# The first queries' low products in full width, and two pieces of W_out in each other's ring

## The chip, the cores and the metric

The kernel runs on one core of a Trainium2 chip. The time is that of one execution on the device, in microseconds (us); three runs of the kernel before gave 1198.80, 1199.49 and 1199.53, the median is 1199.49. Engines are named as in the profile: PE is TensorE's matrix multiplication and PEld its weight loads, DVE is VectorE, ACT is ScalarE, POOL is GpSimd, SP is SyncE, which here issues the DMAs. SBUF is the memory on the chip, PSUM holds the sums of matmuls.

## The reference

Two layers over 1024 tokens of width 1024. Layer 0 pools over trailing windows; layer 1 is a forgetting attention of 16 heads of width 64. Each layer adds a small attention into 256 memory tokens, gates both, projects them with W_out (1536 x 1024) and normalises. The part that the change touches is the attention's second product and the projection behind it:

```python
logits = q @ k.T / 8 + (cum[t] - cum[s])      # causal, 16 heads of width 64
p = softmax(logits)
y_main = p @ v                                # (1024, 1024) over all heads
y = concat([y_main * silu(g_main), y_mem * silu(g_mem)])
x = layer_norm(alpha * x + y @ w_out)         # w_out: 12 row tiles of 128, two column halves of 512
```

All inputs are float32 and the result is held to float32 accuracy, so the kernel splits its operands into a high and a low part and adds up products of parts.

## The kernel before

**The order of work.** The kernel is written for a framework that places waits on semaphores by itself and that plans the order of each engine's queue when the program is built, by its own estimate of every instruction's duration. For TensorE this planning is switched off (`tc.manual_schedule(engines={PE})`): matmuls run in the order in which the code issues them. ACT, DVE, POOL and SP follow the planner. Buffers come in rings: `MK` has 4 buffers of 4 KB a partition, `w` and `wl` have 4 each (high and low parts of weight slabs), `raw` has 4 (weights as they land), `B` 10, `T` 6, and others.

**The heads.** `fox` runs over 16 heads and, in a head, over eight tiles of 128 queries, from the last tile to the first. `probs` (L968 on) makes a tile's logits (`mm3`, L231, into the PSUM ring `L`), DVE adds the forget term and takes the extreme (L986, into a buffer of `MK`), ACT takes the exponential (L994, into the PSUM ring `T`). One step later `halves` makes the probabilities' high part on ACT (L1015) and the low part on DVE (L1016), and `turn` transposes both by DMA (L1028). Between these, `Fill.pump` lets TensorE work on pieces of other projections (`slab`, L253): it is what keeps TensorE busy while the softmax runs.

**The values.** `values(hd, c, o)` multiplies a head's probabilities with its values, once for the queries of tiles 4 to 7 (c = 1) and once for those of tiles 0 to 3 (c = 0, "the first queries"). `v[:, b, 2j]` is the high part of 128 tokens' values (64 columns), `v[:, b, 2j + 1]` the low part. A full product (L1045) loads both, 128 columns, and sends the high part of the probabilities through: one half of the PSUM partitions gets high times high, the other low times high. For the probabilities' low part only the values' high part is needed, 64 columns. So L1051 uses half of the array, alternately the lower and the upper half (`half`), and the two halves of the accumulator are added at the end: ACT takes one half out (L1057), DVE adds the other (L1058). For c = 1 there are 8 + 7 + 6 + 5 = 26 blocks of 128 tokens, for c = 0 there are 4 + 3 + 2 + 1 = 10; each has one full and one half product.

**W_out.** `OutProj` brings W_out in as 12 pieces of 256 x 512, each as two loads of 128 x 512 (`fetch`, L495, into `raw`; some earlier ones into `B`). `split` makes a piece's parts with `hi_lo`: ACT casts the high part (L189), DVE subtracts (L190), ACT, or POOL in the heads, writes the high part once more as bf16 (L196 or L194). `wtags` says in which ring a piece's parts stay: with the tag `w` in two buffers of `w` and four of `wl`, with `MK` in two buffers of `MK`. Pieces 0 to 3 are split during the last heads; `rest` splits pieces 4 to 11 (`self.split(24)`), on DVE behind the eviction of the last head's c = 1 (`tc.issue_after(self.behind)`). Pieces are used in the order 4, 5, 0, 1, 2, 3 of pairs of row tiles; numbers 6 and 7 of the list (the seventh and the eighth) are the two column halves of the second pair of the main branch. `closing`, `products` and `early` issue the matmuls (L540); after `early` the first pair of token tiles takes c = 0 of y, for which pieces 4 to 7 are needed.

Of the kernel before, what the change touches and what calls it, by code (L numbers as in the profile page):

```python
# [99 lines left out]
def trunk_kernel(ctx, tc, x, xT, memT, win, wk, wv0, wv, wmk, wmv, wout, poolw, pscale, lng, lnb, bforget, out):  # L100
# [5 lines left out]
    nc = tc.nc  # L106
# [22 lines left out]
    def ps(shape, tag, bufs):  # L129
        return psum.tile(shape, F32, tag=tag, name=nm(tag), bufs=bufs)  # L130
# [36 lines left out]
    def w_slots(tags, where):  # L167

        def tiles(k):
            tag, bufs = tags[k]  # L170
            if tag == "w":
                his, los = [wt([P, NH]) for _ in range(2)], [tuple(wt([P, NH], BF16) for _ in range(2)) for _ in range(2)]
                return [his, los]
            if tag == "MK":
                hi, lo = halved(MK, [P, 2, NH])
            elif tag == "PP":
                hi, lo = halved(lambda shape, dt=F32R: sb(shape, "P", 5, dt), [P, 2, NH])
            elif tag == "PG":
                hi, lo = sb([P, 2, NH], "P", 5, F32R), duo(sb([P, 2, 2, NH], "G", 4, BF16))
            else:  # L180
                hi, lo = halved(lambda shape, dt=F32R: sb(shape, tag, bufs, dt, where), [P, 2, NH])
            return [[hi[:, j, :] for j in range(2)], [cut(lo, slice(None), j) for j in range(2)]]

        return tiles
# [187 lines left out]
    def mem_attention(l, XH, XL, kv, qtile, ytile, yd):  # L372
# [85 lines left out]
        if True:  # L458
            for t in range(ST + 2):
                part = fill.left / (5 * (ST + 2 - t))  # L460
                if t < ST:
                    probs(t)
                fill.pump(part if t <= ST else 3 * part)
                for h in range(MH):
                    if t >= 3 and t % 2 == 1:
                        values((t - 3) // 2, h)
                    fill.pump(part if t <= ST else part / 2)
            fill.pump(float("inf"))
# [211 lines left out]
    with tc.tile_pool(name="in0", bufs=1) as in0:  # L680
# [58 lines left out]
        wtags = [("B", 8)] * 4 + [("W", 4)] * 2 + [("w", 0), ("MK", 4), ("MK", 4), ("Y", 3), ("PP", 0), ("PG", 0)]  # L739
# [16 lines left out]
    with tc.tile_pool(name="in1", bufs=1) as in1:  # L756
# [262 lines left out]
        pt, homes = {}, {}  # L1019
# [14 lines left out]
        def values(hd, c, o):  # L1034


            (v, un), b = pairs[hd // 2][2], hd % 2
            acc = ps([P, NH], "O", 1)
            blocks = [(i, j) for i in range(4 * c + 3, 4 * c - 1, -1) for j in range(i + 1)]

            def cols(i):
                return slice((i % 4) * P, (i % 4 + 1) * P)

            for n, (i, j) in enumerate(blocks):
                nc.tensor.matmul(  # L1045
                    acc[:, cols(i)], v[:, b, 2 * j : 2 * j + 2, :].rearrange("p e d -> p (e d)"), pt[hd, i][:, j, :],
                    start=n == 0, stop=False, skip_group_check=True,
                )
            for n, (i, j) in enumerate(blocks):
                half = slice(64 * (n % 2), 64 * (n % 2) + 64)  # L1050
                nc.tensor.matmul(  # L1051
                    acc[half, cols(i)], v[:, b, 2 * j, :], pt[hd, i][:, i + 1 + j, :],
                    start=False, stop=n >= len(blocks) - 2, skip_group_check=True,
                )
            own, other = slice(64 * b, 64 * b + 64), slice(64 - 64 * b, P - 64 * b)
            oc = o[own, c * NH : (c + 1) * NH]
            nc.scalar.activation(oc, acc[other, :], AF.Copy, scale=un[own])  # L1057
            return nc.vector.scalar_tensor_tensor(oc, acc[own, :], un[own], oc, ALU.mult, ALU.add).ins  # L1058
# [30 lines left out]
        def fox(following, out_proj):  # L1089
# [8 lines left out]
            for hd in range(HEADS + 1):  # L1098
# [20 lines left out]
                for i in range(ST if hd < HEADS else LAG):  # L1119
# [46 lines left out]
                    if older and older[1] == (4 if older is past[0] else 0):  # L1166
                        last = values(older[0], older[1] // 4, older[2])
                        out_proj.behind = last if older[1] else out_proj.behind
                        if older[0] % 2 and older[1] == 0:
                            finished = pair_out(older[0] // 2, older[2], gs.get(older[0] // 2))  # L1170
# [10 lines left out]
                if b and pr < 7:  # L1181
                    complete(pr + 1)

        wtags = [("B", 10), ("V", 3), ("MK", 4)] + [("B", 10)] * 3 + [("w", 0), ("MK", 4), ("R", 2), ("PP", 0), ("PG", 0), ("B", 10)]
        out_proj = OutProj(1, w_slots(wtags, in1), y1d)
        with tc.manual_schedule(engines={PE}):
            own, (keys, following) = pair_units(0), pair_units(1)
# [66 lines left out]
```

## Time and profile before

| | |
|---|---|
| runs shown | 1198.80, 1199.49, 1199.53 us, median 1199.49 |
| the profiled execution | 1198.79 us, of which the span of its instructions is 1197.0 |
| TensorE's granted clock | 0.999 |
| busy | PE 1172.2, PEld 739.3, DVE 800.5, ACT 616.9, POOL 208.4 us |
| DMA | 182.06 MB, mean 152 GB/s |

A row of the timeline is the start of a group of like instructions in us, the time from its first start to its last end, the engine, the line, the operation, what it writes and reads, its shape and the count; in brackets stand the engine's idle time before it and what ended it. A row of a group by line gives the busy time, the mean of one and the idle time before. A row of the waits says who waited for whom, how long in total, how often, and the longest. Consecutive matmuls overlap in their recorded length, since each passes through the array behind the one before; their rate is read from starts. A few per cent of the matmuls' records are missing from a trace.

### The profile page before, as it was taken

The page shows a single profiled execution, that of the slowest core. Times are in us where ns is not written, and L with a number is a line of the kernel's source. Part 1 is how long each engine was busy: PE and PEld are TensorE (multiplying, and loading weights), DVE is VectorE, ACT ScalarE, POOL GpSimd, SP SyncE. Part 2 cuts the span into 40 slices and gives each one's busy share as a digit, 9 for nine tenths or more (in the row PEclk, how much of TensorE's full clock was granted, in tenths as well). Part 3 has the DMA queues.
Part 4 walks back from the last instruction along what each step waited for, and adds up shares of the span by engine and source line. Part 5 has one row for each costly group of instructions (what it writes and reads, how often), then busy time and mean ns, then how long its engine had stood idle before and what let it go on. Part 6 is the DMA issues. An engine that isn't in the chain of part 4 may idle for free. (4 is left out here: it accounts for less than half of the span.)

```text
span 1197.0 us, 19472 instructions
## 1 busy us (share of the span) xinstructions
PE 1172.2 (98%) x6810; PEld 739.3 (62%) x6927; DVE 800.5 (67%) x1864; ACT 616.9 (52%) x1330; POOL 208.4 (17%) x312
## 2 busy tenths in 40 slices
PE   9999999999999999999999999999999999999997
PEld 4567665555555555677776666666666666655554
DVE  6544767374656576377546888778878888874654
ACT  7433654262532224366325777767766787773110
POOL 2000000000000000200103334333334324530000
PEclk9999999999999999999999999999999999999999
DMA  7333654242355666355526789879897999976431
GB/s 246 115 101 87 131 115 159 79 123 80 102 197 158 159 156 161 106 138 100 171 54 161 152 199 173 195 155 195 187 186 164 195 191 210 230 206 229 154 116 48
DMA packets 280803, 182.06 MB, mean 152 GB/s; under 512 B 225024, under 2 KB 238976, under 8 KB 280704
## 3 DMA queue, kind: packets, MB, share of 16 engines
q1 hardware_dynamic: 280704, 180.81, 62.0%
q8 instruction: 54, 0.88, 0.3%
q14 instruction: 45, 0.37, 0.1%
HBM read 95.24 MB, written 22.61 MB: 98 GB/s over the span
## 5 line engine op out<-in xcount | busy, mean ns | idle before, releaser
L253 PE MATMUL pj<-A,w 128*128 128x512 bf16 (+1 forms) x1817 | 571.4, 398 | 2.2 <-DVE B L894 1.1
L253 PE MATMUL pj<-A,wl 128*128 128x512 bf16 x929 | 351.8, 380 | 6.4 <-issue 3.4
L253 PEld LDWEIGHTS pj<-A,w 128*128 128x128 f32 x944 | 174.8, 188 | 45.4 <-POOL wl L200 2.0
L253 PEld LDWEIGHTS <-w 128*128 128x128 bf16 x960 | 93.1, 98 | 121.3 <-issue 39.4
L253 PEld LDWEIGHTS <-wl 128*128 128x128 bf16 x960 | 94.3, 98 | 87.9 <-issue 4.2
L994 ACT ACTIVATE T<-MK,s 128x512 f32<-128x512 f32 x192 | 111.0, 578 | 44.5 <-DVE s L986 22.6
L1015 ACT ACTIVATE P<-T,s 128x512 f16<-128x512 f32 x192 | 103.1, 576 | 52.8 <-issue 26.3
L1016 DVE SCALAR_TENSOR_TENSOR P<-T,s,P 128x512 f16<-128x512 f32 x192 | 112.3, 612 | 24.0 <-ACT P L1015 22.3
L540 PEld LDWEIGHTS <-T 128*128 128x128 bf16 x736 | 70.6, 98 | 88.9 <-issue 6.8
L190 DVE TENSOR_TENSOR wl<-raw,w 128x512 bf16<-128x512 f32 (+1 forms) x96 | 67.9, 713 | 72.3 <-ACT w L189 69.7
L231 PE MATMUL L<-B,B 128*128 128x512 f32 (+3 forms) x384 | 109.0, 386 | 4.6 <-DVE s L986 4.2
L189 ACT CAST w<-raw 128x512 fp32r<-128x512 f32 (+1 forms) x104 | 62.8, 609 | 84.0 <-PE pj L253 57.6
L231 PEld LDWEIGHTS L<-B,B 128*128 128x128 f32 x384 | 71.1, 189 | 29.6 <-DVE s L986 9.9
L353 POOL TENSOR_SCALAR A<-A 128x1024 bf16<-128x1024 f32 x8 | 8.4, 1049 | 444.5 <-ACT A L351 427.9
L986 DVE CUSTOM_DVE_ANT_0 MK<-L,R 128x512 f32<-128x512 f32 (+3 forms) x128 | 72.8, 569 | 8.4 <-PE L L231 5.6
L978 POOL TENSOR_SCALAR_AFFINE_SELECT R<-R 128x128 f32<-128x128 f32 x128 | 42.2, 335 | 207.4 <-DVE s L986 162.5
L200 POOL TENSOR_TENSOR wl<-raw,w 128x512 bf16<-128x512 f32 x54 | 69.4, 1285 | 3.8
L190 DVE TENSOR_TENSOR T<-T,T 128x1024 bf16<-128x1024 f32 x23 | 31.6, 1374 | 48.1 <-ACT T L189 48.0
L189 ACT CAST T<-T 128x1024 fp32r<-128x1024 f32 x23 | 24.1, 1047 | 71.7 <-DMA T<-y1d 45.4
L199 POOL TENSOR_SCALAR w<-raw 128x512 fp32r<-128x512 f32 x54 | 35.9, 665 | 58.5 <-PE pj L253 58.5
L540 PE MATMUL L<-B,T 128*128 128x512 bf16 (+1 forms) x163 | 43.1, 391 | 0.3
L433 ACT ACTIVATE P<-L,s 128x256 f32<-128x256 f32 x64 | 29.6, 474 | 23.4 <-issue 13.0
(296 smaller groups left out, 1789.7 us busy)
## 6 DMA issues: line engine op xcount, KB each, us to landing
raw<-in_win_dram SPq DMA_DIRECT2D x94, 256.0 KB, 2.9
raw<-in_wout_dram SPq DMA_DIRECT2D x40, 256.0 KB, 2.9
B<-B SPq DMA_DIRECT2D x32, 256.0 KB, 4.5
R<-cumd SPq DMA_DIRECT2D x16, 512.0 KB, 4.6
T<-y0d SPq DMA_DIRECT2D x12, 512.0 KB, 5.1
y0d<-Y SPq DMA_DIRECT2D x11, 512.0 KB, 2.7
T<-y1d SPq DMA_DIRECT2D x11, 512.0 KB, 4.7
raw<-in_wmk_dram SPq DMA_DIRECT2D x16, 256.0 KB, 2.7
```

The source lines that it names most:

```text
L189: pin(nc.scalar.copy(hi, src))
L190: pin(by.tensor_tensor(lo[0], src, hi.bitcast(F32), ALU.subtract))
L199: nc.gpsimd.tensor_scalar(hi, src, 1.0, 1.0, ALU.mult, ALU.mult)
L200: nc.gpsimd.tensor_tensor(lo[0], src, hi.bitcast(F32), ALU.subtract)
L231: nc.tensor.matmul(acc, a, b, start=i == 0, stop=i == len(terms) - 1)
L253: nc.tensor.matmul(acc, a, b, start=start, stop=stop)
L540: nc.tensor.matmul(acc, y, w, start=c == 2 and j == firsts[id(acc)] and acc is not self.seeded, stop=c == 1 and j == lasts[id(acc)], skip_ ...
L978: nc.gpsimd.affine_select(R[:, qs], R[:, qs], [[-1, P]], ALU.is_ge, -NEG, base=0, channel_multiplier=1).ins
L986: nc.vector.tensor_tensor_reduce(p[:, lo:up], lg, R[:, lo:up], 1.0, top, ALU.add, ALU.min, m[:, n : n + 1])
L994: nc.scalar.activation(e, p[:, lo:up], AF.Exp, bias=top, scale=-1.0, accum_out=sums[:, n, hd % 2, i : i + 1],)
L1015: nc.scalar.activation(pair[:, lo:up], e, AF.Copy, scale=r)
L1016: nc.vector.scalar_tensor_tensor(pair[:, L + lo : L + up], e, r, pair[:, lo:up], ALU.mult, ALU.subtract)
```

## The change

Two edits. In `values`, for c = 0 only, the ten half products are replaced by ten full ones: both parts of the values are loaded and the probabilities' low part passes through all 128 columns, so the low part times the low part is added too. For c = 1 the half products stay. In `wtags`, the seventh and the eighth entry change places.

```diff
-            for n, (i, j) in enumerate(blocks):
+            if c == 0:
+                for n, (i, j) in enumerate(blocks):
+                    nc.tensor.matmul(
+                        acc[:, cols(i)], v[:, b, 2 * j : 2 * j + 2, :].rearrange("p e d -> p (e d)"),
+                        pt[hd, i][:, i + 1 + j, :], start=False, stop=n == len(blocks) - 1, skip_group_check=True,
+                    )
+            for n, (i, j) in enumerate(blocks if c else ()):
                 half = slice(64 * (n % 2), 64 * (n % 2) + 64)
                 nc.tensor.matmul(
                     acc[half, cols(i)], v[:, b, 2 * j, :], pt[hd, i][:, i + 1 + j, :],
...
-        wtags = [("B", 10), ("V", 3), ("MK", 4)] + [("B", 10)] * 3 + [("w", 0), ("MK", 4), ("R", 2), ("PP", 0), ("PG", 0), ("B", 10)]
+        wtags = [("B", 10), ("V", 3), ("MK", 4)] + [("B", 10)] * 3 + [("MK", 4), ("w", 0), ("R", 2), ("PP", 0), ("PG", 0), ("B", 10)]
```

## The prediction

> **What bounds the kernel now.** I read the page's head first, then the busy time by stage, then TensorE's waits in the two stages that the change touches.
>
> ```profile
> span 1197.0 us, 19472 instructions
> ...
> PE 1172.2 (98%) x6810; PEld 739.3 (62%) x6927; DVE 800.5 (67%) x1864; ACT 616.9 (52%) x1330; POOL 208.4 (17%) x312
> ```
> ```profile
> core 0: us, PE busy (x) PEld busy (x) DVE busy (x) ACT busy (x) POOL busy (x), PEclk, DMA share, GB/s
> 660.00:1070.00 410.00, 398.99 (x2730) 262.91 (x2776) 334.18 (x947) 298.43 (x687) 159.43 (x253) 1.00 0.92 189
> ```
>
> TensorE is busy 98% of the span. The sixteen heads of the attention run from about 660 to 1070 us, the rest of the output projection follows. In the heads' stage VectorE is busy 334 of 410 us and ScalarE 298, so the softmax is close behind TensorE. TensorE's waits, first in the heads' stage (us in total, times, longest), then from 1070 us on:
>
> ```profile
> PE L L231 <- DVE s L986: 4.2, 9, 1.0
> PE pj L253 <- issue: 3.8, 24, 0.2
> PE pj L253 <- DVE B L894: 1.1, 2, 0.5
> ```
> ```profile
> PE L L540 <- DVE MK L190: 0.8, 2, 0.5
> ```
>
> So TensorE waits 4.2 + 1.1 = 5.3 us for the softmax and the evictions in 410 us, and 0.8 us for one weight piece later. The row with 24 waits for "issue" belongs mostly to the blocks that the change touches; I come to it first.
>
> **The change part by part. (a) What one block of a head costs now.** Three rows of the timeline of matmuls (start, length, line, count), with what comes after, show one block of the first queries, c = 0: ten full products (L1045), ten half products (L1051), then projection work:
>
> ```profile
> 699.45 0.72 PE L1045 MATMUL O<-T,V 128*128 128x128 f16 x10
> 700.10 0.47 PE L1051 MATMUL O<-T,V 128*64 128x128 f16 x10
> 700.73 0.38 PE L253 MATMUL pj<-A,wl 128*128 128x512 bf16 x1 [0.16 <-issue]
> 700.95 0.38 PE L253 MATMUL pj<-A,w 128*128 128x512 bf16 x1
> ```
> ```profile
> L1045 PE MATMUL O<-T,V x576: 219/219/230, 663.6 to 1069.1; 128*128 128x128 f16 x192
> ```
>
> One full product lasts 0.219 us and ten in a row end after 0.72, so they start (0.72 - 0.22) / 9 = 0.0556 us apart. Ten half products end after 0.47: (0.47 - 0.22) / 4 = 0.06 from pair to pair, two at a time. A half product therefore costs half of a full one, but changing over costs too: from the first full to the first half product it is 0.65 us, not 10 x 0.056 = 0.56, so 0.09 goes into the change, and more into the way back.
>
> How much, the rows just shown seem to say: the next matmul starts at 700.73, that is 1.28 us after the block's first, with 0.16 us of idle time. Twenty full products take 20 x 0.0556 = 1.11. That would be a gain of 0.17 us a block. I don't believe it, because of the weight loads of the same stretch:
>
> ```profile
> 700.10 0.31 PEld L1051 LDWEIGHTS <-V 128*64 128x64 f16 x10
> 700.50 0.10 PEld L253 LDWEIGHTS <-w 128*128 128x128 bf16 x1
> 700.51 0.10 PEld L253 LDWEIGHTS <-wl 128*128 128x128 bf16 x1
> 700.73 0.10 PEld L253 LDWEIGHTS <-w 128*128 128x128 bf16 x1
> ```
>
> Each load belongs to one matmul, and in steady work a load starts as the matmul before it starts (700.73 in both lists). Here two loads, w at 700.50 and wl at 700.51, precede the matmul of 700.73, which is the one with wl. The matmul with w has no record; it started at about 700.51 and filled the 0.22 us up to 700.73. The idle 0.16 us is a lost record. The page counts 6927 loads and 6810 matmuls, so 117 are lost in all, and the last head's block, where nothing is missing, confirms the length:
>
> ```profile
> 1068.55 0.73 PE L1045 MATMUL O<-T,V 128*128 128x128 f16 x10
> 1069.21 0.47 PE L1051 MATMUL O<-T,V 128*64 128x128 f16 x10
> 1069.61 0.50 PE L540 MATMUL pj<-MK,B 128*128 128x512 f32 x1
> ```
>
> 1069.61 - 1068.55 = 1.06 us, and 700.51 - 699.45 = 1.06 us. With the changed line a block is 1.11 us: **+0.05 us a block**. Sixteen heads have one such block each: +0.8 us of TensorE time at most. The Trainium skill, TensorE: Matmul & The Clock Gate, Part 3, says that column tiles run side by side, their matmuls starting some 4 ns apart. By that rule alone, with no price for the changes of mode, the five saved slots would come back whole. The trace agrees with the pairs and shows the changes as well.
>
> In rows, giving back the pairs alone would be 5 x 0.056 = 0.28 us a block, 4.5 us in all; the 1.06 us already holds both, so I give that sum a small chance.
>
> The extra term (low part of the values times low part of the probabilities) costs nothing else: the same weights are loaded, the same number of instructions issued, the accumulator and its two evictions (L1057, L1058) stay. They come 0.05 us later, and what is queued behind them on ScalarE and VectorE with them. No DMA is added or moved on SP's queue, and nothing on POOL's.
>
> **(b) What of the 0.8 us is kept.** Where TensorE waits for the softmax afterwards, later arrival only shortens the wait, if VectorE's chain did not itself wait for TensorE. It seldom did:
>
> ```profile
> DVE MK L986 <- PE L L231: 1.4, 4, 0.4
> DVE MK L986 <- PE O L1051: 0.7, 4, 0.2
> ```
>
> 2.1 us in eight waits, against TensorE's 5.3 in eleven. The last of TensorE's waits on the softmax, and the blocks of first queries behind it:
>
> ```profile
> 1011.72 0.50 PE L231 MATMUL L<-B,B 128*128 128x256 f32 x2 [0.17 <-DVE s L986]
> ...
> 1016.30 0.72 PE L1045 MATMUL O<-T,V 128*128 128x128 f16 x10
> ...
> 1045.37 0.72 PE L1045 MATMUL O<-T,V 128*128 128x128 f16 x10
> ```
>
> With the block at 1068.55 three blocks, 0.15 us, have no such wait behind them, and the thirteen before them, 0.65 us, meet 5.3 us of waits. So between +0.1 and +0.8 us arrive at 1070; I take the middle, +0.4.
>
> **(c) The two rings.** Pieces seven and eight of W_out (numbers 6 and 7 of the list) swap places. Both are split in the same way: two casts, two low parts on VectorE, two copies on ScalarE; the count doesn't change. The place matters by when its last reader is done and by where the planner then puts the instructions. Last readers: the last projection matmul with wl, and the last exponential from MK; then the first writes:
>
> ```profile
> 1056.46 0.38 PE L253 MATMUL pj<-A,wl 128*128 128x512 bf16 x1
> ```
> ```profile
> 1058.46 0.36 ACT L994 ACTIVATE T<-MK,s 128x128 f32<-128x128 f32 x1
> ...
> 1068.72 1.04 ACT L189 CAST T<-T 128x1024 fp32r<-128x1024 f32 x1 [2.72 <-DMA T<-y1d]
> 1069.67 1.21 ACT L189 CAST w<-raw 128x512 fp32r<-128x512 f32 x2
> 1070.78 1.13 ACT L196 CAST wl<-w 128x512 bf16<-128x512 f32 x2
> 1071.94 0.68 ACT L1057 ACTIVATE G<-O,unscale 64x512 f32<-64x512 f32 x1
> 1072.65 1.14 ACT L189 CAST MK<-raw 128x512 fp32r<-128x512 f32 x2
> ```
>
> Both rings are free over 10 us before the first write, so neither wait is what holds the pieces: the first is behind the cast of y and its own load, the second behind the eviction. With the order unchanged the swap is worth nothing, and the wait on "MK" becomes one on "wl". If the planner moves the eighth piece's work ahead of the eviction (0.68 us on ScalarE, 0.76 on VectorE), TensorE's two waits vanish, -0.8. If a cast of y (1.04) slips in front instead, they grow by that, +1.0. Here are those waits and VectorE's rows:
>
> ```profile
> 1074.19 0.59 PE L540 MATMUL L<-MK,T 128*128 128x512 bf16 x2 [0.30 <-DVE MK L190]
> 1075.32 0.59 PE L540 MATMUL L<-MK,T 128*128 128x512 bf16 x2 [0.54 <-DVE MK L190]
> ```
> ```profile
> 1071.09 1.29 DVE L190 TENSOR_TENSOR wl<-raw,w 128x512 bf16<-128x512 f32 x2
> 1072.66 0.76 DVE L1058 SCALAR_TENSOR_TENSOR G<-O,unscale,G 64x512 f32<-64x512 f32 x1 [0.28 <-ACT G L1057]
> 1073.45 1.83 DVE L190 TENSOR_TENSOR MK<-raw,MK 128x512 bf16<-128x512 f32 x2
> ```
>
> I take 0, nearest to the rows as they stand; the ends are -0.8 and +1.0. The last block's own 0.05 us is inside these waits.
>
> **(d) The order of the queues.** ScalarE, VectorE, POOL and SP get their order from a planner that works with its own durations. Sixteen blocks with other matmuls can tip it anywhere from the first head on. No row shows that. The nearest bound is what TensorE waits for the softmax now: all of it gone is -5.3 us, doubled is +5.3. I take 0 and keep the ends.
>
> **Sum:** the profiled execution took 1198.79 us (span 1197.0 and 1.79 around it); +0.4 +0 +0 gives 1199.2. The median of the three runs shown, 1199.49, is 0.70 above it, so the forecast is **1199.9 us**, which is no difference that a measurement can tell: 0.2%, 2.4 us, is about the least that can be told for this kernel.
>
> **The rivals.**
>
> *Slower: another order of the queues in the heads.* It is a single mechanism: an eviction or a projection's cast of about 0.7 us (0.76 for L1058 above) stands ahead of a softmax step that TensorE waits for. TensorE's eleven waits of that kind are 5.3 / 11 = 0.48 us each now. Five more of them are 2.4 us, the point from which this decides; one more in every second head is 8 x 0.48 = +3.8, so 1203.7. For it speaks how close VectorE is, 334 of 410 us; against it that TensorE's own order is written out by hand and stays. A chance of 0.25, and 0.02 more for the pairs' whole price, 1199.5 + 4.5 = 1204.0.
>
> *Faster: the idle 0.16 us is real.* Then fifteen blocks gain 1.28 - 1.11 = 0.17 and the last loses 0.05: -2.5 us against the median, 1197.0. The loads and the last block speak against it; a chance of 0.07. The Trainium skill, TensorEngine Tiling, Key Properties, says that a change of tiling mode drains the engine; it gives no length. By that rule removing two changes a head gains, and the trace agrees that a change costs something (0.09 us on the way in).
>
> *Faster: a better order.* The two waits after 1074 vanish (-0.8) and half of the 5.3 us (-2.6): 1199.9 - 3.4 = 1196.5. A chance of 0.11.
>
> *The change does nothing:* the forecast without its 0.4, 1199.5, which can't be told from it.
>
> **How the numbers follow.** The forecast, with its own range of 1198.9 (order kept, nothing arrives, and the waits at 1074 shorter) to 1201.3 (all of the 0.8 us and +1.0 at the rings), has 0.55. Slower than +0.2% is 0.25 + 0.02 = 0.27, faster is 0.07 + 0.11 = 0.18. The range that leaves out no more than 2 in 10 takes in the idle-time rival at 1197.0 and the other order up to its price: 1196.9 to 1203.7.
>
> **What would show it.** In the changed kernel's rows a block of c = 0 is one group of twenty L1045-like products over 1.11 us, from its first start to the start of the next load; no half products remain there, and the "issue" row loses fifteen waits of 0.16 us without the span getting shorter by 2.5. The 26-product blocks (c = 1) keep their changes. The count of lost records falls by about fifteen. TensorE's waits for L986 stay near 4.2 us; if they are 7 or more, the other order holds. After 1070 us the waits on MK L190 appear as waits on wl L190, 0.8 us together. The prediction is wrong if the next load follows the twenty products later than 0.06 us after the last, if the queues' order in the heads is another one, or if piece eight's low parts come ahead of L1058.

## The result and the profile after

The changed kernel takes **1202.09 us** (median of 13 runs, 1201.88 to 1202.75), the kernel before 1199.40 (13 runs, 1198.46 to 1199.91). The ratio is 1.0025, 95% interval 1.0017 to 1.0032: slower by 2.7 us. The time lies in the predicted range, 1196.9 to 1203.7, but the likeliest case, no difference, did not happen; the rival "another order of the queues in the heads" did, by another mechanism than the rival had. The profiled execution took 1202.43 us.

Behind the edit all lines are 6 higher: the half products are L1057 now, ScalarE's and VectorE's evictions of the values L1063 and L1064, and L1051 is the new full product with the probabilities' low part. The page's head, the stage of the heads and TensorE's waits (us in total, times, longest) of the changed kernel:

```profile
span 1200.6 us, 19478 instructions
...
PE 1174.8 (98%) x6810; PEld 743.3 (62%) x6927; DVE 799.4 (67%) x1864; ACT 616.3 (51%) x1330; POOL 207.6 (17%) x312
```
```profile
660.00:1070.00 410.00, 398.85 (x2703) 264.63 (x2749) 332.33 (x945) 296.26 (x685) 158.44 (x253) 1.00 0.92 186
```
```profile
PE L L231 <- DVE s L986: 6.4, 13, 1.3
PE pj L253 <- issue: 1.9, 12, 0.2
PE L L540 <- DVE wl L190: 1.1, 1, 1.1
PE pj L253 <- DVE B L894: 1.1, 2, 0.5
PE L L540 <- DVE MK L190: 0.3, 1, 0.3
```

The clock is the same. TensorE waits 6.4 us for the softmax where it waited 4.2, in 13 places instead of 9, and 1.4 us instead of 0.8 at the weights of the output projection. The first and the last start of the full products show where the time went (columns: shortest, median and longest duration in ns, then first and last start in us):

```profile
L1045 PE MATMUL O<-T,V x576: 219/219/230, 663.6 to 1071.7; 128*128 128x128 f16 x192
```

Before, they ran from 663.6 to 1069.1. In the heads 2.6 us are lost by this row, 2.70 from the start of the first block to the start of the last. The two profiled executions differ by more than the medians, 3.64 us; the other 1.0 us lies behind the start of the last block (129.46 us to the end of the span instead of 128.46).

VectorE shows what happens there. Its waits in the heads' stage, before and after:

```profile
DVE P L1016 <- ACT P L1015: 22.3, 40, 1.1
```
```profile
DVE P L1016 <- ACT P L1015: 25.4, 46, 1.1
```

Six more waits and 3.1 us more for one thing: the high part of the probabilities from ScalarE, from which VectorE makes the low part. The first new one is 0.47 us at 690 us. The second, the longest of the six, is shown here on VectorE's timeline, before and then after:

```profile
696.27 0.16 DVE L1007 RECIPROCAL s<-s 128x1 f32<-128x1 f32 x1
696.46 0.69 DVE L894 TENSOR_TENSOR B<-pj,B 64x512 fp32r<-64x512 f32 x1
697.18 0.56 DVE L986 CUSTOM_DVE_ANT_0 MK<-L,R 128x384 f32<-128x384 f32 x1
697.66 0.08 DVE L986 DVE_READ_ACCUMULATOR2_ANT s<- 128x1 f32 x1
697.66 1.27 DVE L1016 SCALAR_TENSOR_TENSOR P<-T,s,P 128x512 f16<-128x512 f32 x2
```
```profile
696.11 0.16 DVE L1007 RECIPROCAL s<-s 128x1 f32<-128x1 f32 x1
697.07 1.28 DVE L1016 SCALAR_TENSOR_TENSOR P<-T,s,P 128x512 f16<-128x512 f32 x2 [0.81 <-ACT P L1015]
698.38 0.68 DVE L894 TENSOR_TENSOR B<-pj,B 64x512 fp32r<-64x512 f32 x1
699.09 0.56 DVE L986 CUSTOM_DVE_ANT_0 MK<-L,R 128x384 f32<-128x384 f32 x1
```

Before, the eviction of a key projection (L894) and the next tile's extreme (L986) filled the time that ScalarE needs for L1015. Now L1016 stands ahead of both and VectorE idles 0.81 us. ScalarE's queue is turned in the same way there: its cast of the same projection (L893) ran at 695.44 and runs at 697.40 now, behind L1015. TensorE feels it at 720:

```profile
720.45 0.50 PE L231 MATMUL L<-B,B 128*128 128x256 f32 x2 [0.80 <-DVE s L986]
```

A second kind of flip comes in four heads, the first at 727 us. Before and after:

```profile
727.84 0.74 DVE L1058 SCALAR_TENSOR_TENSOR G<-O,unscale,G 64x512 f32<-64x512 f32 x1
728.51 0.99 DVE L1016 SCALAR_TENSOR_TENSOR P<-T,s,P 128x384 f16<-128x384 f32 x2
```
```profile
729.03 1.01 DVE L1016 SCALAR_TENSOR_TENSOR P<-T,s,P 128x384 f16<-128x384 f32 x2 [0.39 <-ACT P L1015]
729.96 0.73 DVE L1064 SCALAR_TENSOR_TENSOR G<-O,unscale,G 64x512 f32<-64x512 f32 x1
```

The eviction of the first queries' values, which had covered ScalarE's copy, stands behind L1016 now, and VectorE idles 0.39 us. It was ready, since ScalarE's part of it ended at 727.70 + 0.69 = 728.39:

```profile
727.70 0.69 ACT L1063 ACTIVATE G<-O,unscale 64x512 f32<-64x512 f32 x1
```

TensorE's new wait after it:

```profile
738.65 0.62 PE L231 MATMUL L<-B,B 128*128 128x384 f32 x2 [0.47 <-DVE s L986]
```

On VectorE the first kind at 697 and the second in four heads add up to 0.81 + 4 x 0.39 = 2.4 us, which is about the loss in the heads. With the 0.47 us at 690 it is 2.8, but TensorE's next wait, at 695 us, fell from 0.65 to 0.39. The Trainium skill, Perfetto Trace Analysis, section Tensor Engine Instruction, says of ScalarE's, VectorE's and GpSimd's queues that they are "strict FIFO". These rows agree: the ready L1064 behind the waiting L1016 does not overtake it.

### The profile page after: what moved, and what is told of

The parts are those of the page before. It is cut to its first block, busy times and chain, and to the rows that moved or that the text cites. A ratio compares the mean times of both kernels' runs of the same rounds, so it can differ in the third digit from the quotient of the medians.

```text
span 1200.6 us, 19478 instructions
## 1 busy us (share of the span) xinstructions
PE 1174.8 (98%) x6810; PEld 743.3 (62%) x6927; DVE 799.4 (67%) x1864; ACT 616.3 (51%) x1330; POOL 207.6 (17%) x312
## 5 line engine op out<-in xcount | busy, mean ns | idle before, releaser
L253 PE MATMUL pj<-A,w 128*128 128x512 bf16 (+1 forms) x1817 | 571.5, 398 | 1.6 <-DVE B L894 1.1
L253 PE MATMUL pj<-A,wl 128*128 128x512 bf16 x929 | 351.9, 380 | 5.5 <-issue 1.9
L253 PEld LDWEIGHTS pj<-A,w 128*128 128x128 f32 x944 | 174.9, 189 | 45.2 <-POOL wl L200 2.0
L253 PEld LDWEIGHTS <-w 128*128 128x128 bf16 x960 | 93.1, 98 | 120.4 <-issue 39.4
L253 PEld LDWEIGHTS <-wl 128*128 128x128 bf16 x960 | 94.2, 98 | 87.4 <-issue 4.0
L1015 ACT ACTIVATE P<-T,s 128x512 f16<-128x512 f32 x192 | 103.1, 577 | 54.6 <-issue 27.9
L1016 DVE SCALAR_TENSOR_TENSOR P<-T,s,P 128x512 f16<-128x512 f32 x192 | 112.2, 612 | 27.1 <-ACT P L1015 25.4
L231 PE MATMUL L<-B,B 128*128 128x512 f32 (+3 forms) x384 | 109.2, 387 | 6.4 <-DVE s L986 6.4
L231 PEld LDWEIGHTS L<-B,B 128*128 128x128 f32 x384 | 71.1, 189 | 31.6 <-DVE s L986 11.8
L978 POOL TENSOR_SCALAR_AFFINE_SELECT R<-R 128x128 f32<-128x128 f32 x128 | 42.4, 337 | 213.9 <-DVE s L986 168.2
L986 DVE CUSTOM_DVE_ANT_0 MK<-L,R 128x512 f32<-128x512 f32 (+3 forms) x128 | 72.7, 568 | 7.9 <-PE L L231 5.0
```

Source lines behind the costliest of these rows:

```text
L231: nc.tensor.matmul(acc, a, b, start=i == 0, stop=i == len(terms) - 1)
L253: nc.tensor.matmul(acc, a, b, start=start, stop=stop)
L978: nc.gpsimd.affine_select(R[:, qs], R[:, qs], [[-1, P]], ALU.is_ge, -NEG, base=0, channel_multiplier=1).ins
L986: nc.vector.tensor_tensor_reduce(p[:, lo:up], lg, R[:, lo:up], 1.0, top, ALU.add, ALU.min, m[:, n : n + 1])
L1015: nc.scalar.activation(pair[:, lo:up], e, AF.Copy, scale=r)
L1016: nc.vector.scalar_tensor_tensor(pair[:, L + lo : L + up], e, r, pair[:, lo:up], ALU.mult, ALU.subtract)
```

## The experiments

Theory O: the order of the queues costs the time, and the planner chose another one because it puts another duration on the new products. Rival M: the products themselves cost it. Rival R: the rings do. In the tables "heads" is the time from the start of the first L1045 block (c = 1 of the first head) to the start of the last block of first queries, in the profiled execution; it is 404.92 us before and 407.62 after. It comes from one execution of each kernel; where two kernels below differ only in the rings, it agrees within 0.1 us.

**Each edit alone.** The first run keeps the old `wtags`, the second the half products:

```diff
-        wtags = [...] + [("B", 10)] * 3 + [("MK", 4), ("w", 0), ("R", 2), ...]
+        wtags = [...] + [("B", 10)] * 3 + [("w", 0), ("MK", 4), ("R", 2), ...]
```

> The full products of c = 0 alone; W_out's pieces seven and eight stay in the rings of the kernel before. The order of VectorE's, ScalarE's, POOL's and SP's queues in the heads is then the changed kernel's, the order behind the heads that of the kernel before. Theory O (the queues' order costs: the starts of the c = 0 blocks are 2.64 us later by head 15 in the changed kernel's profile): about +2.6 us, 1202.0, with TensorE's waits for L986 at 6.4 us as in the changed kernel. Rival M (the matmuls themselves cost more than 0.05 us a block): the same +2.6 here, so this run does not part O from M. Rival R (the rings cost it all): +0.0 to +0.3, and the waits for L986 at 4.2 us.

```diff
-            if c == 0:
+            if c < 0:
...
-            for n, (i, j) in enumerate(blocks if c else ()):
+            for n, (i, j) in enumerate(blocks):
```

> The swap of the two rings alone; c = 0 keeps its half products, so that the queues' order differs from the kernel before only behind the heads (pieces seven and eight of W_out are interleaved with the last evictions). O and M: +0.6 us, the growth of TensorE's waits at L540 behind 1070 us in the changed kernel's profile (1.46 against 0.84 us), 1200.0. R: about +2.7, 1202.1.

**Products and order apart.** An edge of order queues an instruction behind another one of its engine, without a wait. Such edges between neighbours, wherever the two kernels' queues differ, give the full products the order of before (all four queues are then the same, instruction by instruction), and in the fourth run the half products the changed kernel's order in the heads:

```diff
         out_proj.rest(x1, None, None, out)
+    by = {i.name: i for i in nc.cur_bb.bb.instructions}
+    for names in ORDER:
+        for first, then in zip(names, names[1:]):
+            tc.add_manual_dep(by[then], first, mybir.DependencyInfo(mybir.DependencyClass.NoSync, ...), ...)
...
+ORDER = [
+    ['I-6878', 'I-6977', 'I-6960', 'I-6962', 'I-6979', 'I-6965', 'I-6967', 'I-7002', 'I-7004'],
...
+    ['I-7449', 'I-7417', 'I-7419', 'I-7482', 'I-7470', 'I-7508', 'I-7471', 'I-7510', 'I-7511'],
...
+]
```

> The full products of c = 0 in the old rings, with all queues held in the order of the kernel before by edges of order alone. O: what is left is the price of the products, 0.05 us a block and at most 0.8 in all: +0.2 to +0.8, 1199.6 to 1200.2, with the waits for L986 back at about 4.2 us and no wait at 720 us. M: +2.6 stays, 1202.0.

> The half products of the kernel before, in its rings, with all queues of the heads held in the changed kernel's order. O: the order costs without the products: +1.8 to +2.6, 1201.2 to 1202.0, waits for L986 at 6 us or more. M: +0.0, 1199.4.

Measured, against 1199.07 us of the kernel before (33 runs):

| kernel | median us | ratio, 95% interval | heads us |
|---|---|---|---|
| products alone, planner's order | 1201.81 | 1.0022, 1.0014 to 1.0031 | 407.55 |
| rings alone | 1199.39 | 1.0001, 0.9993 to 1.0010 | 404.94 |
| products, order of before | 1199.22 | 1.0002, 0.9993 to 1.0011 | 405.22 |
| half products, new order | 1201.65 | 1.0019, 1.0010 to 1.0027 | 407.12 |

TensorE's waits for the softmax go with the order and not with the products; here the products in the order of before, then the half products in the new order:

```profile
PE L L231 <- DVE s L986: 4.0, 9, 1.0
```
```profile
PE L L231 <- DVE s L986: 6.8, 13, 1.3
```

M and R fall: the products cost 0.30 us of the heads where the queues stay as they were, the order 2.20 without any new product. In the whole time the products in the order of before are even a little below the 1199.6 to 1200.2 that I had expected. The weight loads, of which every trace holds all 6927, show the places. The first and the third run have the same products; from the start of the first block to the start of the last the planner's order adds 2.38 us between successive loads of L231, of 2.33 us in all: 0.92 at 719 us and 0.33 to 0.40 at each of 737, 845, 952 and 1002 make 2.43. So TensorE's loss in the heads lies at these five places. Why the planner chose this order is not shown: it does so with the new products alone and not with the new rings alone, but no run shows the durations that it puts on them.

R's swap gives nothing that can be told. The +0.6 that I had expected of it came from reading the changed kernel's waits behind 1070 us as the rings' work. From the start of the last block to the end it is 128.4 to 128.5 us in the three kernels with the old order in the heads (before, rings alone, products in the order of before) and 129.0 to 129.5 in those with the new one (after, products alone, half products). TensorE's listed waits there part less clearly: 0.6 to 1.1 us with the old order, 1.2 to 1.7 with the new one. How the heads' order makes this stretch longer stays open.

**Which flips.** Both runs have the full products in the old rings. In the first, four edges put the eviction L1064 of four heads back ahead of L1016; in the second, the order of before is held only at the key evictions:

```diff
+ORDER = [
+    ['I-7449', 'I-7417'],
+    ['I-9034', 'I-9002'],
+    ['I-10615', 'I-10583'],
+    ['I-11370', 'I-11338'],
+]
```

> The full products of c = 0 in the old rings, in the changed kernel's order, but with the c = 0 eviction of four heads put back ahead of the two P steps (four edges of order). Theory I (VectorE idles 0.38 us at each of these four places, because the P step now stands first and ScalarE's copy for it isn't ready, and the rest of the head is that much later): four times 0.36 us less than with the products alone (1201.81), about 1200.4, with the waits for L986 at about 5.0 us. Rival J (the four places are only where the delay shows, and its cause is the flip at 696 us): no change, 1201.8.

```diff
+ORDER = [
+    ['I-6878', 'I-6977', 'I-6960', 'I-6962', 'I-6979', 'I-6965', 'I-6967', 'I-7002', 'I-7004'],
...
+    ['I-6954', 'I-6978', 'I-6993', 'I-6961', 'I-6963', 'I-6980', 'I-7000', 'I-6995', 'I-6996', 'I-7042'],
+]
```

> The same, but with the four evictions left behind the P steps and the order of the kernel before put back only between 685 and 700 us (key evictions of head 2 ahead of the P steps, ScalarE and VectorE). Theory I: the idle 0.80 us of VectorE at 696 us and TensorE's wait at 720 us vanish, 0.85 us less than with the products alone, about 1201.0, waits for L986 about 5.6 us. Rival J: all of the 2.6 us vanish, 1199.2.

| kernel | median us | ratio, 95% interval | heads us |
|---|---|---|---|
| four evictions back | 1200.11 | 1.0008, 0.9999 to 1.0017 | 405.96 |
| key evictions back | 1200.75 | 1.0014, 1.0005 to 1.0023 | 406.68 |

The kernel before has 1199.18 here (27 runs). Against the products alone (407.55) the heads get 1.59 us back from the four edges and 0.87 from the other; together 2.46, where the whole old order gave 2.33. With the four edges TensorE's waits at 738, 847 and 1005 us are gone, with the others the one at 720. The two kinds add, so one is not the other's shadow, and rival J of the expectations falls. Nothing is left for the few other places where the queues differ in the heads (on VectorE at 760, 868 and 1051 us, on POOL at 969).

**The price of the products, made larger.** All sixteen heads' products are full, for c = 1 too, in the old rings and in the order of before, but for one pair on VectorE at 1051 us and ScalarE's order behind the heads:

```diff
-            if c == 0:
+            if c >= 0:
...
-            for n, (i, j) in enumerate(blocks if c else ()):
+            for n, (i, j) in enumerate(()):
```

> Full products for c = 1 too (52 products at 0.056 us a block, 2.90 us, where 26 and 26 halves took 2.39), with the queues of the heads in the order of the kernel before. The block's price is then 0.51 us in each of sixteen heads and 0.06 in each c = 0 block, 9.1 us in all. If TensorE alone sets the pace, all of it arrives but what its waits for the softmax take up (4.2 us): +5 to +9, 1204 to 1208. If, as the c = 0 blocks showed, a third arrives: +3, 1202.

1201.32 us, ratio 1.0018 (1.0009 to 1.0027): +2.1 of a price of 9.1 us, less than either case that I had expected. The waits of TensorE take most of it up:

```profile
PE L L231 <- DVE s L986: 0.9, 2, 0.5
```

Against the run with only c = 0 full, in the same order, the price is 16 x 0.51 = 8.2 us, and 1201.32 - 1199.22 = 2.1 arrive; 6.1 are missing. The row falls by only 3.1 us, from 4.0. But a listed wait is counted from the modelled end of the matmul before. By the weight loads, which have the same sequence in both traces, the time between successive loads of L231 falls by 5.6 us in sum; with 0.2 at L894 (1.1 to 0.9) 0.3 us stay unexplained. The Trainium skill, Perfetto Trace Analysis, section Tensor Engine Instruction, says that TensorE's end times are "a model, not a measurement". The two counts of one wait agree with that.

**An order better than both.** Before, too, an eviction stands in the way: L1064 waits for ScalarE, with a ready L986 behind it for which TensorE waits. At fourteen places L986 goes first; further edges hold the rest of VectorE's order. ScalarE's, POOL's and SyncE's queues still differ from those of before in two places each (ScalarE at 1049 and 1060 us, the others at about 812 and 920); TensorE's loads do not shift there. Half products and old rings are kept:

```diff
+ORDER = [
+    ['I-6951', 'I-6937'],
+    ['I-7332', 'I-7318'],
+    ['I-7717', 'I-7702'],
...
+    ['I-12067', 'I-12053'],
...
+]
```

> The kernel before with its half products and rings, and with fourteen evictions L1064 (L1058 of the kernel before) put behind the next L986 on VectorE, which TensorE waits for; the rest of VectorE's order is held. Theory I: the waits for L986 at 695, 746, 827, 854, 935, 961 and 1011 us (0.64, 0.18, 0.40, 0.16, 0.41, 0.41, 0.17) vanish, and perhaps the two for L894 (0.53 each) with them: -1.5 to -3 us, 1196.1 to 1197.6. If what the eviction held up comes late in its place: 1199 or more.

**1194.42 us**, ratio 0.9961 (0.9949 to 0.9974): 4.8 us less than the kernel before, more than I expected, and faster than both kernels. The heads are 4.3 us shorter. One of the places, in the run of the rings alone (whose heads have the order of before) and here:

```profile
744.42 0.76 DVE L1064 SCALAR_TENSOR_TENSOR G<-O,unscale,G 64x512 f32<-64x512 f32 x1 [0.93 <-ACT G L1063]
745.21 0.69 DVE L986 CUSTOM_DVE_ANT_0 MK<-L,R 128x512 f32<-128x512 f32 x1
```
```profile
743.25 0.68 DVE L986 CUSTOM_DVE_ANT_0 MK<-L,R 128x512 f32<-128x512 f32 x1
...
744.26 0.76 DVE L1064 SCALAR_TENSOR_TENSOR G<-O,unscale,G 64x512 f32<-64x512 f32 x1 [0.33 <-ACT G L1063]
```

The idle 0.93 us shrinks to 0.33, and L986 comes 2.0 us earlier. TensorE's waits for the softmax and the last full product:

```profile
PE L L231 <- DVE s L986: 2.8, 4, 0.8
```
```profile
L1045 PE MATMUL O<-T,V x576: 216/219/230, 663.6 to 1064.7; 128*128 128x128 f16 x192
```

The listed waits for L986 fall by only 1.4 us, from 4.2, and those for L894 by 0.7. By the weight loads, counted as above, 4.2 of the 4.3 us are between loads of L231: up to 0.9 us is gained at a place, and 0.7 and 0.4 us are lost again at 737 and 1002 us.

**Each edit on the better order.** With the queues held as in that run, first the full products of c = 0, then the swap of the rings:

> The full products of c = 0 in the old rings, with every queue held in the order of the run with the fourteen evictions behind L986 (1194.42). The products' price, 0.062 us in fifteen blocks, is 0.9 us. If it arrives more as TensorE waits less for the softmax (2.8 us here against 4.2): +0.5 to +0.9, 1194.9 to 1195.3. If a fifth to a third of it arrives, as in the order of the kernel before: +0.2 to +0.3, 1194.7. In no case is the change a gain: were the half products' changes of mode dearer than shown, 1193.5 or less.

> The swap of the two rings alone, on the same better order, half products kept. If TensorE's two waits at L540 for the pieces' low parts (0.65 and 0.54 us) go with it: -0.5 to -1.2, 1193.2 to 1193.9. If another of the pieces' casts comes late in their place, as in the run of the rings alone (one wait of 0.64): within 0.5 of 1194.4.

1195.06 us (ratio 0.9968, 0.9956 to 0.9981) and 1195.30 us (0.9966, 0.9952 to 0.9979), against 1194.42; the intervals overlap that run's. The products' +0.6 is as expected. The rings' +0.9 is not: it lies outside both cases. The heads are 400.94 and 400.70 us, against 400.64: the products cost 0.30 us of the heads again, the rings nothing. The waits for the pieces' parts, 1.2 us in the better order, did not vanish with the new rings (1.3 and 0.5 us), and from the start of the last block to the end it is 129.2 us instead of 128.6. Neither edit is a gain in the better order.

## Why the prediction was right or wrong

The range held because it took in the rival up to its price. The forecast itself, no difference, failed at (d), and the rival's size was met by another mechanism than its own; that part is luck.

*(a) The price of a block: right, a little small.* Two runs whose traces have all matmuls show a block of first queries, with half products (the rings alone) and with full ones (order of before):

```profile
673.35 0.72 PE L1045 MATMUL O<-T,V 128*128 128x128 f16 x10
674.00 0.47 PE L1057 MATMUL O<-T,V 128*64 128x128 f16 x10
674.40 0.39 PE L253 MATMUL pj<-A,w 128*128 128x512 bf16 x1
```
```profile
673.57 0.72 PE L1045 MATMUL O<-T,V 128*128 128x128 f16 x10
674.13 0.72 PE L1051 MATMUL O<-T,V 128*128 128x128 f16 x10
674.69 0.38 PE L253 MATMUL pj<-A,w 128*128 128x512 bf16 x1
```

1.05 and 1.12 us: +0.06 where I had +0.05, in fifteen blocks 0.9 us. In these rows no idle time stands before L253. "The same weights are loaded" was not so: the half products load 128x64, the full ones 128x128, and PEld is busy for 743.3 us instead of 739.3. What that costs is within the 0.06 us.

*The idle 0.16 us is not real: right.* The run of the rings alone keeps the half products and its page counts 6927 matmuls, as many as loads; there the row for "issue" is gone from the waits, and the time is that of the kernel before.

*(b) What arrives: right.* +0.4 expected, +0.30 in the heads measured, twice (405.22 against 404.92, 400.94 against 400.64). The middle of +0.1 to +0.8 was a guess; that it came so near is luck too.

*(c) The rings: right in size, 0, in the old order of the heads.* The order behind the heads was not kept, though I had assumed it: the pieces' casts are interleaved with the last evictions, and in the changed kernel one of piece eight's two low parts is made ahead of L1064, at 1075.38 us, which I had named as a sign of being wrong. It came to nothing all the same: the two waits became one of 0.64 us in the run of the rings alone. "0.8 together" on wl was wrong: 1.1 on wl and 0.3 on MK in the changed kernel. The run of the rings alone has the same queues behind the heads, so the rise comes with the order in the heads.

*(d) "I take 0" for the order of the queues: this step failed.* It is worth 2.2 to 2.3 us of the heads, nearly all of the loss, where my ends were -5.3 and +5.3. I wrote that sixteen blocks with other matmuls can tip the planner anywhere and then set the likeliest value to nothing because no row showed it. The rival had the size: five of TensorE's waits are new or clearly longer (0.80 us at 720, 0.47 at 738, 0.44 at 847, 1.30 at 955 where 1.01 stood at 953, 0.44 at 1005), 2.4 us in sum, "the point from which this decides". But it had the mechanism the wrong way round. I had an eviction or a cast slipping in ahead of a softmax step. What happened is that they went behind one: L1016 came to stand first while ScalarE's copy for it was still to be made, and the evictions that had filled VectorE's time meanwhile were behind it. My own picture, an eviction ahead of L986, was there already, in fourteen places of the kernel before; taking it away is worth 4.8 us, 4.3 of them in the heads.

*What would show it.* The twenty products over 1.11 us came. The fifteen waits of 0.16 us are gone: twelve in the "issue" row and three that were listed as waits for POOL (L978 twice, L1083). So only half of that row's 24 belonged to the changed blocks, not most; the other twelve stand behind c = 1 and are still there. The count of lost records did not fall: 117 again. Waits for L986 of "7 or more" were to mean another order; 6.4 with another order shows that I set this point too high. The queues' order in the heads, named as a sign of being wrong, is another one. The next product follows the last one of the block after 0.056 us, as forecast. The intervals of 11 to 13 runs reach about 0.1% to either side, so less than the 0.2% that I gave as the least can be told.

## What to carry to other kernels

Where a planner orders the queues, a change on one engine can also change the others' order, even if it hardly alters that engine's time: compare the queues before reading the time, and hold the old order by edges to see the change itself. In an in-order queue look for rows with idle time whose successor is ready, above all a wait on a neighbour engine with a step behind it that the busiest engine waits for; here fourteen such swaps were worth 4.8 us, the products 0.3. Time added to an engine that is 98% busy arrives only where it does not wait next for another: 2.1 of 9.1 us did.

## What was not expected of the hardware

The traces come in two kinds, with all 6927 matmuls or with exactly 117 fewer. The kind does not follow c = 0: with half products there it is 6927 (rings alone) and 6810 (before), with full ones 6927 (products alone) and 6810 (after). It went with the group of runs: the first four runs lost none, the next four lost 117 each, the last two none. Each kernel has one trace, so what decides it stays open. The fastest order, one of the traces with 6810, has idle rows for "issue" too (3.4 us in 21 waits); the same order with full products, with all 6927, has none, so they are no time that can be won.
